# Sharing the attention normalisation between two engines, and taking the context rows of the MLP into products of quarters

## The chip, the cores and the metric

One core of one Trainium2 chip runs the whole program. The core has a matrix engine (TensorE; PE in the profile, with PEld for its weight loads), two engines for elementwise work (VectorE, shown as DVE, and ScalarE, shown as ACT), GpSimd (POOL), and SyncE (SP), which issues the DMAs. The metric is the device time of one execution in microseconds, the median over repeated runs.

## What is computed

Two layers of a hybrid transformer block over 512 latent tokens and 256 context tokens of width 1024. Cut to the two places that the change touches:

```python
# attention, per block of 128 query tokens; 8 query heads on 2 key/value heads, head size 64
p = softmax(concat([s_lat, s_ctx, s_sink], -1))           # keys: up to 3 latent blocks of 128, 2 context blocks
out = p_lat @ v_window + p_ctx @ v_ctx
...
# MLP, for the 512 latent rows in both layers, for the 256 context rows in layer 0 alone
f = square(relu(t @ w1)) @ w2                              # w1: 1024 x 4096, w2: 4096 x 1024
```

All matrix products run to single-precision accuracy by splitting: an operand x becomes a rounded part hi and a remainder lo = x - hi, and a product takes three matmuls, hi*hi + hi*lo + lo*hi.

## The kernel before, in words

The program is written in one order, and a planner then places the instructions of each engine: it follows the program with estimated costs and puts on each engine what is ready by them; of several that are ready it doesn't always take the one that stands first in the program. What it fixes is each engine's order; on the chip an engine executes that order and waits where an operand isn't there.

**Attention** (`phase_a`). A unit is one block of 128 query tokens with one key/value head, so four query heads. Layer 0 has 12 units (two context blocks first, then four latent ones), layer 1 has 8. `attn_scores` makes the four heads' scores in PSUM, adds the mask and takes the row maximum on VectorE (L936), takes exp with row sums on ScalarE (L944), then forms 1/sum on VectorE (L946, L947) and scales the four score tiles by it on VectorE (L949). `attn_values` transposes the scaled tiles on TensorE (L962), copies the transposed blocks from PSUM to the SBUF tile `pts`, on ScalarE for even and VectorE for odd blocks (L963; a ScalarE copy shows as L569, the line of the helper), and multiplies them with the values (L969). `pts` is one tile of up to five blocks in one buffer. Scores have two buffers a head (`np3` = 8), and the values of a unit run one unit behind its scores (`vlag` = 1). The output projection of finished blocks (`pass0`, and the products of `mm3`, L640 to L642) fills TensorE between them.

**MLP of layer 0** (`phase_mlp`). The 4096 hidden columns are worked in 8 groups of 512. Groups 3 to 6 are `strassen(g)`. There `up` makes the hidden tile of one 128-column chunk c, for the latent rows (24 matmuls of 512 columns) and the context rows (24 of 256). Then the down-projection of the latent rows runs as seven products of quarters in place of eight: `w2_forms` makes sums and differences of the four quarters of w2 and splits them (L666, L671, L672), `h_forms` does the same for the quarters of the latent hidden tile (L699, L700, L706 to L708, L712), and `times` multiplies a pair (L1507 to L1509, 12 matmuls of 512 columns), accumulating in the PSUM banks X, Y, Z, and adds the bank to the result `facc` (L1516) before the next product goes on in the same bank. The context rows go another way: `up` splits them (L1480, L1481) and `plain` multiplies them with the four quarters of w2 as they are, 24 matmuls and two adds (L1492) for each half of the columns. One `plain` stands ahead of the products X and Y, the other behind Y. The quarters of w2 live in 10 weight tiles that the w1 blocks of the group also use, so a form of w2 is made only when `up` or an earlier product gives tiles back.

## Time and profile before

| | |
|---|---|
| median of 3 runs | 1626.89 us (1626.73 to 1628.28) |
| the profiled execution | 1627.44 us, of which the trace spans 1625.7 us |
| TensorE busy | 1522.6 us, 94% |
| VectorE busy | 1078.5 us, 66% |
| ScalarE busy | 639.2 us, 39% |
| attention of layer 0, of layer 1 (about) | 245 to 362 us, 1155 to 1236 us |
| groups 3 to 6 of the MLP of layer 0 (about) | 635 to 907 us |

A busy TensorE isn't TensorE at its peak, since matmuls are pipelined and their ends are modelled; how much work fits in a stretch is read from the distance between the starts of matmuls. The share of busy time is a mean over stages with different limits, so each stage has to be read by itself.

### The profile page before, as it was taken

How to read it: one execution, taken by the hardware profiler on the slowest of the kernel's cores; microseconds unless marked ns; L12 is line 12 of the kernel's file. 1: busy time of each engine (PE TensorE's matmuls, PEld its weight loads, DVE VectorE, ACT ScalarE, POOL GpSimd, SP SyncE). 2: the span in 40 equal slices, each digit the busy share in tenths (PEclk: the TensorE clock that was granted, in tenths of full speed). 3: DMA queues.
4: the chain of work that ended last, by engine and by line, in shares of the span. 5: the costliest groups of instructions: out<-in, count | busy, mean ns of one | idle time of the engine just before them, and what ended most of it. 6: DMA issues, size and time to landing. Idle time of an engine off the chain costs nothing.

```text
span 1625.7 us, 22752 instructions
## 1 busy us (share of the span) xinstructions
PE 1522.6 (94%) x8740; PEld 1232.8 (76%) x8740; DVE 1078.5 (66%) x2288; ACT 639.2 (39%) x1199; POOL 188.0 (12%) x185
## 2 busy tenths in 40 slices
PE   5899999899999999999999997999889799999997
PEld 2677776667888888887888875688677688888885
DVE  8766638667885472647466476563763878879785
ACT  5411235654523121443334344122463564445441
POOL 0000121002312110000000135003201100000012
PEclk9999999999999999999999998879999899999999
DMA  9366412005232253042230347743302243232312
GB/s 346 120 209 207 151 46 79 1 21 187 73 134 93 76 178 100 29 132 102 106 130 2 121 186 295 266 143 93 117 1 104 104 155 104 89 119 85 123 59 84
DMA packets 72765, 193.82 MB, mean 119 GB/s; under 512 B 14928, under 2 KB 25424, under 8 KB 72272
## 3 DMA queue, kind: packets, MB, share of 16 engines
q1 hardware_dynamic: 68208, 188.17, 33.3%
q10 hardware_dynamic: 4448, 4.19, 0.8%
q8 instruction: 69, 1.13, 0.3%
q14 instruction: 40, 0.33, 0.1%
HBM read 172.15 MB, written 20.19 MB: 118 GB/s over the span
## 4 chain that ended last, share of the span: by engine, by line
PE 79%; DVE 11%; DMA 4%; ACT 4%; issue 1%; SPq 0%; POOL 0%; DVEq 0%; ACTq 0%
PE ps_m L640 15%; PE ps_m L641 15%; PE ps_m L642 15%; PE ps_q L1507 4%; PE ps_q L1508 4%; PE ps_q L1509 4%; PE ps_a L827 3%; PE ps_q L641 3%; PE ps_q L640 3%; PE ps_q L642 3%; ACT p L944 2%; PE ps_s L526 2%; DVE p L936 1%; PE ps_t L969 1%; DVE p L949 1%
## 5 line engine op out<-in xcount | busy, mean ns | idle before, releaser
L623 ACT CAST w<-w 128x1024 fp32r<-128x1024 f32 x128 | 133.8, 1049 | 221.6 <-PE ps_q L641 72.5
L641 PE MATMUL ps_m<-g,w 128*128 128x256 f32 (+1 forms) x544 | 178.6, 330 | 0.0
L640 PE MATMUL ps_m<-g,w 128*128 128x256 f32 (+1 forms) x544 | 177.0, 330 | 1.2 <-DVE g L784 1.2
L624 POOL TENSOR_TENSOR w<-w 128x1024 fp32r<-128x1024 f32 x33 | 80.6, 2443 | 839.4 <-ACT w L623 411.9
L642 PE MATMUL ps_m<-g,w 128*128 128x256 f32 (+1 forms) x544 | 177.5, 328 | 0.0
L641 PE MATMUL ps_m<-f,w 128*128 128x512 f32 (+1 forms) x464 | 170.0, 367 | 0.3 <-POOL f L787 0.3
L642 PE MATMUL ps_m<-f,w 128*128 128x512 f32 (+1 forms) x464 | 170.2, 368 | 0.0
L640 PE MATMUL ps_m<-f,w 128*128 128x512 f32 (+1 forms) x464 | 170.2, 371 | 0.0
L624 DVE TENSOR_TENSOR w<-w 128x1024 fp32r<-128x1024 f32 x95 | 120.1, 1267 | 74.8 <-ACT w L623 68.2
L640 PE MATMUL ps_m<-w,f 128*128 128x512 f32 (+1 forms) x400 | 147.6, 373 | 8.9 <-DVE p L989 4.0
L642 PE MATMUL ps_m<-w,f 128*128 128x512 f32 (+1 forms) x400 | 147.7, 370 | 0.0
L641 PE MATMUL ps_m<-w,f 128*128 128x512 f32 (+1 forms) x400 | 146.8, 368 | 0.0
L1516 DVE TENSOR_TENSOR g<-g,ps_q 128x512 f32<-128x512 f32 x146 | 93.4, 681 | 31.3 <-PE ps_q L1509 30.9
L641 PEld LDWEIGHTS ps_m<-g,w 128*128 128x128 f32 x544 | 104.0, 191 | 11.2 <-issue 1.2
L640 PEld LDWEIGHTS ps_m<-g,w 128*128 128x128 f32 x544 | 103.2, 192 | 11.7 <-DVE g L784 1.5
L642 PEld LDWEIGHTS ps_m<-g,w 128*128 128x128 f32 x544 | 103.8, 191 | 9.5 <-DVE w L624 0.4
L640 PEld LDWEIGHTS ps_m<-f,w 128*128 128x128 f32 x464 | 88.8, 193 | 19.6 <-issue 6.2
L642 PEld LDWEIGHTS ps_m<-f,w 128*128 128x128 f32 x464 | 88.9, 192 | 17.7 <-issue 4.5
L641 PEld LDWEIGHTS ps_m<-f,w 128*128 128x128 f32 x464 | 88.8, 191 | 14.6 <-DVE ssm_tab L303 1.2
L640 PEld LDWEIGHTS ps_m<-w,f 128*128 128x128 f32 x400 | 75.9, 190 | 22.7 <-issue 3.6
L640 PE MATMUL ps_q<-w,f 128*128 128x512 f32 x224 | 87.7, 395 | 2.3 <-DVE g L1682 2.0
L641 PE MATMUL ps_q<-w,f 128*128 128x512 f32 x224 | 87.8, 393 | 0.0
(319 smaller groups left out, 3256.3 us busy)
## 6 DMA issues: line engine op xcount, KB each, us to landing
w<-in_w_ada SPq DMA_DIRECT2D x72, 512.0 KB
w<-in_w_mlp_in SPq DMA_DIRECT2D x64, 512.0 KB
w<-in_w_mlp_out SPq DMA_DIRECT2D x36, 512.0 KB
wr<-in_w_mlp_out SPq DMA_DIRECT2D x14, 1024.0 KB
ada_w<-in_w_ada SPq DMA_DIRECT2D x21, 512.0 KB
w<-in_w_out SPq DMA_DIRECT2D x16, 512.0 KB
w<-in_w_conv SPq DMA_DIRECT2D x12, 512.0 KB
h_d<-g SPq DMA_DIRECT2D x12, 512.0 KB
```

The lines of the kernel that those rows point to most:

```text
L526: nc.tensor.matmul(out(g), U[d].o[rows, q, k].rearrange("p t i -> p (t i)"), sp[d][rows, q, k, lo:NCH], start=False, stop=d == 1 and q == ...
L623: nc.scalar.copy(hi, raw)
L624: (nc.gpsimd if turn % 2 and E.wpool and pool else nc.vector).tensor_sub(lo, raw, hi.bitcast(F32))
L640: nc.tensor.matmul(out, lh, rh, start=first, stop=False)
L641: nc.tensor.matmul(out, lh, rl, start=False, stop=False)
L642: nc.tensor.matmul(out, ll, rh, start=False, stop=last)
L827: nc.tensor.matmul(pa[32 * b:32 * b + 32, k * 256:(k + 1) * 256], E.cT[:, kc], raw[k][:, b * 256:(b + 1) * 256], start=kc == 0 and k == 0, ...
L944: nc.scalar.activation(p[i][:, :nk * P], p[i][:, :nk * P], AF.Exp, bias=nm[:, i:i + 1], accum_out=sm[:, i:i + 1])
L1507: nc.tensor.matmul(o, f[:, 0, c, js], rh[:, c], start=first and c == 0, stop=False, **kw)
L1508: nc.tensor.matmul(o, f[:, 0, c, js], rl[:, c], start=False, stop=False, **kw)
L1509: nc.tensor.matmul(o, f[:, 1, c, js], rh[:, c], start=False, stop=c == 1, **kw)
L1516: V.tensor_add(a_, a_, b_)
```

## The change

Three edits. In `attn_scores` the odd two of a unit's four tiles are scaled on ScalarE, the even two stay on VectorE. In `attn_values` each transposed block has a tile of its own, from nine buffers. In groups 3 to 6 of the MLP the context rows go through the same seven products as the latent rows: `h_forms` is run a second time on the context hidden tile (quarters of 128 rows), `times` makes a product of 6 matmuls for them behind each latent one, in a bank from the tag 'm' of three, and adds it to `facc`; `plain`, the split in `up` and the form r12 of w2 go. `up` now makes the latent rows of a chunk first. The new forms live in a pool that takes the place of the pool `prep`, whose work is drained first.

```diff
...
 
 
-def w2_forms(E, views, ctx):
+def w2_forms(E, views):
 
...
     yield "r11", split((0, 0))
     yield "r21", split((1, 0))
-    if ctx:
-        yield "r12", split((0, 1))
     yield "r22", split((1, 1))
...
 
 
-def h_forms(E, hf):
+def h_forms(E, hf, n, end, alloc):
 
 
     nc = E.nc
     V = nc.vector
-    q = {(i, j): hf[j][:, :, i * 256:(i + 1) * 256] for i in range(2) for j in range(2)}
+    q = {(i, j): hf[j][:, :, i * n:(i + 1) * n] for i in range(2) for j in range(2)}
 
     def split(x):
-        f = E.f4([P, 2, 2, 256], F32R)
+        f = alloc([P, 2, 2, n], F32R)
         nc.scalar.copy(f[:, 0], q[x])
         V.tensor_sub(f[:, 1], q[x], f[:, 0].bitcast(F32))
         return f
 
-    yield "l11", split((0, 0))
-    yield "l12", split((0, 1))
-    yield "l22", split((1, 1))
+    yield "l11" + end, split((0, 0))
+    yield "l12" + end, split((0, 1))
+    yield "l22" + end, split((1, 1))
     V.tensor_add(q[1, 1], q[1, 0], q[1, 1])
     V.tensor_sub(q[1, 0], q[0, 0], q[1, 0])
     V.tensor_sub(q[0, 0], q[1, 1], q[0, 0])
-    yield "s2", split((0, 0))
-    yield "s1", split((1, 1))
-    yield "s3", split((1, 0))
+    yield "s2" + end, split((0, 0))
+    yield "s1" + end, split((1, 1))
+    yield "s3" + end, split((1, 0))
     V.tensor_sub(q[0, 1], q[0, 1], q[0, 0])
-    yield "s4", split((0, 1))
+    yield "s4" + end, split((0, 1))
 
...
     V.reciprocal(sm, sm)
     for i in range(4):
-        V.tensor_scalar(out=p[i][:, :nk * P], in0=p[i][:, :nk * P], scalar1=sm[:, i:i + 1], scalar2=None,
-                        op0=OP.mult)
+        if i % 2:
+            nc.scalar.mul(p[i][:, :nk * P], p[i][:, :nk * P], sm[:, i:i + 1])
+        else:
+            V.tensor_scalar(out=p[i][:, :nk * P], in0=p[i][:, :nk * P], scalar1=sm[:, i:i + 1], scalar2=None,
+                            op0=OP.mult)
     return p, keys
...
     V = nc.vector
     nk = len(keys)
-    pts = E.ap.tile([P, 5, 512], F32, name="pts", tag="pts", bufs=1)
+    pts = []
     for j in range(nk):
         pt = E.pt('t')
         for i in range(4):
             nc.tensor.transpose(pt[:, i * P:(i + 1) * P], p[i][:, j * P:(j + 1) * P], E.ident)
-        (V.tensor_copy if j % 2 else E.copy)(pts[:, j], pt)
+        pts.append(E.ap.tile([P, 512], F32, name="pts", tag="pts", bufs=9))
+        (V.tensor_copy if j % 2 else E.copy)(pts[j], pt)
     po = E.pt('t')
     for j in range(nk):
         vv = v[:, keys[j], kv * 64:(kv + 1) * 64]
-        pr = pts[:, j].rearrange("p (a e t) -> p a e t", a=2, e=2)
+        pr = pts[j].rearrange("p (a e t) -> p a e t", a=2, e=2)
         for e in range(2):
...
         phase_a(E, l, cols, st)
     with psum_phase(E, f"m{l}", m=3, a=1, q=2) as E.pp, \
-            tc.tile_pool(name=f"mlp{l}", bufs=1, reuse_waits="tile") as E.g4p, \
-            tc.tile_pool(name=f"prep{l}", bufs=1, reuse_waits="tile") as E.mp:
+            tc.tile_pool(name=f"mlp{l}", bufs=1, reuse_waits="tile") as E.g4p, ExitStack() as E.late:
+        E.mp = E.late.enter_context(tc.tile_pool(name=f"prep{l}", bufs=1, reuse_waits="tile"))
         E.ps, E.nb4 = 'a', 2
...
         S = Env()
         S.hf = [E.f4([P, 2, NL]) for _ in range(2)]
-        S.hx = [E.f4([P, 4, NCX], F32R) for _ in range(2)] if both else None
+        if both:
+            hx = E.f4([P, 4, NCX])
+            S.hx = [hx[:, 2 * j:2 * j + 2] for j in range(2)]
         S.w, S.F = [], {}
...
         s = E.g4p.tile([P, 512], F32, name="relu", tag="relu", bufs=2)[:, :n]
         nc.scalar.activation(s, pt, AF.Relu)
-        nc.scalar.activation(s if sg else S.hf[c // 2][:, c % 2, ts], s, AF.Square)
-        if sg:
-            nc.scalar.copy(S.hx[0][:, c], s)
-            V.tensor_sub(S.hx[1][:, c], s, S.hx[0][:, c].bitcast(F32))
-
-    def plain(S, hf):
-
-        cs = slice(hf * 512, (hf + 1) * 512)
-        for t in (4, 5):
-            js = slice((t % 4) * P, (t % 4 + 1) * P)
-            pt = E.pt('m')
-            for c in range(4):
-                r = S.F[f"r{c // 2 + 1}{hf + 1}"]
-                mm3(nc, pt, S.hx[0][:, c, js], S.hx[1][:, c, js], r[0][:, c % 2], r[1][:, c % 2], c == 0, c == 3)
-            V.tensor_add(facc[t][:, cs], facc[t][:, cs], pt)
+        nc.scalar.activation((S.hx if sg else S.hf)[c // 2][:, c % 2, ts], s, AF.Square)
 
     begun = set()
 
     def times(S, bank, l, r, first, i, n):
 
         cs = slice(n * 512, (n + 1) * 512)
-        if bank not in S.F:
-            S.F[bank] = E.pt('q')
-        f, (rh, rl) = S.F[l], S.F[r]
-        for th in range(2):
-            o = S.F[bank][:, th * 512:(th + 1) * 512]
-            js = slice(th * P, (th + 1) * P)
+        rh, rl = S.F[r]
+
+        def product(o, f, js):
             kw = dict(skip_group_check=True)
             for c in range(2):
                 nc.tensor.matmul(o, f[:, 0, c, js], rh[:, c], start=first and c == 0, stop=False, **kw)
                 nc.tensor.matmul(o, f[:, 0, c, js], rl[:, c], start=False, stop=False, **kw)
                 nc.tensor.matmul(o, f[:, 1, c, js], rh[:, c], start=False, stop=c == 1, **kw)
-        for th in range(2):
-            t = 2 * i + th
+
+        def add(t, b_):
             if t not in facc:
                 facc[t] = E.g4([P, D])
-            a_, b_ = facc[t][:, cs], S.F[bank][:, th * 512:(th + 1) * 512]
+            a_ = facc[t][:, cs]
             if (t, n) in begun or both:
                 V.tensor_add(a_, a_, b_)
             else:
                 V.tensor_copy(a_, b_)
                 begun.add((t, n))
 
+        if bank not in S.F:
+            S.F[bank] = E.pt('q')
+        parts = [S.F[bank][:, th * 512:(th + 1) * 512] for th in range(2)]
+        for th in range(2):
+            product(parts[th], S.F[l], slice(th * P, (th + 1) * P))
+        for th in range(2):
+            add(2 * i + th, parts[th])
+        if both:
+            if bank + "c" not in S.F:
+                S.F[bank + "c"] = E.pt('m')
+            product(S.F[bank + "c"], S.F[l + "c"], slice(0, P))
+            add(4 + i, S.F[bank + "c"])
+
     def forms(S, g, n):
 
         if n:
-            S.R, S.L = w2_forms(E, w2[g * 4:g * 4 + 4], both), h_forms(E, S.hf)
-        for x in (S.R, S.L):
+            S.R, S.L = w2_forms(E, w2[g * 4:g * 4 + 4]), [h_forms(E, S.hf, 256, "", E.f4)]
+            if both:
+                lx = lambda s, d: E.mp.tile(s, d, name="lx", tag="lx", bufs=6)
+                S.L.append(h_forms(E, S.hx, 128, "c", lx))
+        for x in [S.R] + S.L:
             for k in range(n or 9):
...
             next(prep, None)
         for c in range(4):
+            up(S, c, 0)
             up(S, c, 1)
-            up(S, c, 0)
         forms(S, g, 3)
         forms(S, g, 0)
-        plain(S, 0)
         times(S, "X", "l11", "r11", True, 0, 0)
         times(S, "Y", "l12", "r21", True, 0, 0)
-        plain(S, 1)
         late_products(S)
...
             continue
         if l == 0 and g in E.fast:
+            if g == E.fast[0]:
+                drain(prep)
+                E.late.close()
+                E.mp = E.late.enter_context(E.tc.tile_pool(name="lx", bufs=1, reuse_waits="tile"))
             strassen(g)
```

## Rows read from the trace of the kernel before

**Rows 1.** The page: busy time of two engines, and the chain that ended last.
```profile
PE 1522.6 (94%) x8740; PEld 1232.8 (76%) x8740; DVE 1078.5 (66%) x2288; ACT 639.2 (39%) x1199; POOL 188.0 (12%) x185
PE 79%; DVE 11%; DMA 4%; ACT 4%; issue 1%; SPq 0%; POOL 0%; DVEq 0%; ACTq 0%
```

**Rows 2.** Busy time by stretch: length, then PE, PEld, DVE, ACT, POOL, clock, DMA.
```profile
245.00:362.00 117.00, 105.37 (x653) 79.70 (x652) 85.06 (x244) 68.68 (x181) 13.75 (x9) 0.97 0.11 35
1155.00:1236.00 81.00, 72.29 (x460) 55.11 (x460) 57.08 (x152) 47.41 (x119) 5.26 (x4) 0.96 0.11 40
637.00:668.50 31.50, 31.50 (x184) 26.49 (x183) 8.55 (x13) 12.24 (x26) 0.00 (x0) 1.00 0.31 101
668.50:706.00 37.50, 37.50 (x184) 29.77 (x183) 31.20 (x49) 16.59 (x27) 0.00 (x0) 1.00 0.25 85
```

**Rows 3.** Chain that ended last, by line: 245 to 365, 1150 to 1240.
```profile
by line: ACT p L944 15.4%; PE ps_t L969 11.9%; DVE p L936 10.5%; DVE p L949 9.6%; PE ps_t L962 5.5%; PE ps_m L642 4.2%; issue 4.2%; PE ps_m L640 4.1%; PE ps_m L641 3.8%; DVE pts L963 3.4%; DVE qs L911 2.8%; PE ps_q L932 2.3%; PE ps_q L934 2
by line: DVE p L936 12.3%; DVE p L949 10.8%; ACT p L944 10.7%; PE ps_t L969 9.6%; PE ps_t L962 8.8%; DVE pts L963 5.1%; PE ps_m L640 5.1%; PE ps_m L642 4.4%; PE ps_m L641 4.1%; DVE qs L911 3.8%; PE ps_q L932 3.8%; issue 3.2%; PE ps_q L933 2
```

**Rows 4.** One unit in order of time, VectorE: start, length, instruction, idle before.
```profile
319.99 0.16 DVE L941 TENSOR_TENSOR st<-st,nsink 128x4 f32<-128x4 f32 x1
...
323.48 0.16 DVE L946 TENSOR_TENSOR st<-st 128x4 f32<-128x4 f32 x1 [0.52 <-ACT p L944]
...
325.25 1.94 DVE L949 TENSOR_SCALAR p<-p,st 128x640 f32<-128x640 f32 x4
...
330.27 0.16 DVE L941 TENSOR_TENSOR st<-st,nsink 128x4 f32<-128x4 f32 x1
```

**Rows 5.** Groups on VectorE by shape, 245 to 365: count, busy us, mean ns, idle.
```profile
L949 DVE TENSOR_SCALAR p<-p,st 128x512 f32<-128x512 f32 x16 | 6.7, 480 | 0.1
```

**Rows 6.** Scaling by a column on ScalarE elsewhere: ns min/median/max, starts, forms.
```profile
L1207 ACT ACTIVATE f<-f,vecs x6: 510/722/723, 110.8 to 1061.1; 128x512 f32<-128x512 f32 x4, 128x256 f32<-128x256 f32 x2
L745 ACT ACTIVATE g<-g,rs x10: 1132/1140/1154, 393.8 to 997.5; 128x1024 f32<-128x1024 f32 x10
```

**Rows 7.** What VectorE's copies to pts (L963) waited for, whole run: us, times.
```profile
  PE ps_t L962: 15.4, 19
```

**Rows 8.** Waits of TensorE in 1140 to 1240: us in total, times, longest.
```profile
PE ps_q L932 <- DVE st L936: 4.5, 6, 1.7
PE ps_t L962 <- DVE pts L963: 2.5, 4, 0.8
```

**Rows 9.** Matmuls of 512 columns in order of time, ten starts apart.
```profile
784.43 0.39 PE L640 MATMUL ps_m<-f,w 128*128 128x512 f32 x1
...
786.69 0.39 PE L641 MATMUL ps_m<-f,w 128*128 128x512 f32 x1
```

**Rows 10.** Groups 3 to 6 by line (590 to 960): ns min/median/max, starts, forms.
```profile
L641 PE MATMUL ps_m<-w,f x64: 389/389/499, 668.7 to 886.2; 128*128 128x512 f32 x64
L1481 DVE TENSOR_TENSOR f<-relu,f x16: 421/425/428, 640.4 to 866.3; 128x256 fp32r<-128x256 f32 x16
```

**Rows 11.** VectorE in the products of group 3, in order of time.
```profile
669.12 1.29 DVE L672 TENSOR_TENSOR w<-w 128x512 fp32r<-128x512 f32 x2 [4.17 <-ACT w L671]
...
676.85 1.28 DVE L1516 TENSOR_TENSOR g<-g,ps_q 128x512 f32<-128x512 f32 x2
678.06 1.28 DVE L672 TENSOR_TENSOR w<-w 128x512 fp32r<-128x512 f32 x2
...
688.28 0.68 DVE L1492 TENSOR_TENSOR g<-g,ps_m 128x512 f32<-128x512 f32 x1
...
690.98 1.28 DVE L1516 TENSOR_TENSOR g<-g,ps_q 128x512 f32<-128x512 f32 x2 [2.02 <-PE ps_q L1509]
```

**Rows 12.** TensorE there: end of `up`, end of `plain`, first s2 matmul.
```profile
668.27 0.39 PE L642 MATMUL ps_m<-f,w 128*128 128x512 f32 x1
...
685.38 0.39 PE L642 MATMUL ps_m<-w,f 128*128 128x512 f32 x1
...
686.26 0.49 PE L1507 MATMUL ps_q<-w,f 128*128 128x512 f32 x1
```

## The prediction

> **What bounds the kernel now.** The page comes first: TensorE is busy for 94% of the span and carries 79% of the chain that ended last [rows 1]. So time is only to be had where TensorE does less work, or where it now stands idle. The busy time by stretch says where that is [rows 2]. In groups 3 to 6 of the MLP TensorE has no idle time (31.50 of 31.50 us, 37.50 of 37.50 us); there only fewer matmuls help. In the attention stretches it is idle for 117.00 - 105.37 = 11.6 us in layer 0 and 81.00 - 72.29 = 8.7 us in layer 1; these 20.3 us are the most that attention can give. The same view shows the danger: VectorE is nearly empty while `up` runs (8.55 of 31.50 us) and nearly full while the products run (31.20 of 37.50 us).
>
> What holds TensorE up in attention is read from the chain within the two stretches [rows 3]: it goes to and fro between the exps on ScalarE (L944), the maxima on VectorE (L936) and the scaling on VectorE (L949). L949 holds 9.6% of 120 us and 10.8% of 90 us, 11.5 + 9.7 = 21.2 us. One unit shows why [rows 4]. From the end of one L941 to the next is 10.28 us: the exps follow the first of them, L946 follows the last exp at 323.48, the scaling takes 1.94 us from 325.25, and only behind it in VectorE's queue come the next unit's last maxima, L941 and its exps. In layer 1 TensorE waits longest for those maxima (4.5 us), then for the copies to `pts` (2.5 us) [rows 8].
>
> **The change, part by part.**
>
> **Scaling on two engines.** A unit's four scalings take 1.94 us on VectorE where five key blocks are read, 0.485 us each [rows 4]; with four blocks an instruction is 0.48 us long by itself [rows 5]. Two of four go, so VectorE gets through a unit 0.97 us sooner with five blocks and about 0.85 with four. Over the 16 latent units that is some 14.5 us of VectorE time. The chain's own share says less: half of L949's 21.2 us is 10.6 us. I take 10.6 as the upper end. ScalarE gets two instructions a unit that no row shows in this place; the nearest are scalings by a column elsewhere, 0.72 us for 512 columns and 1.14 us for 1024 [rows 6], so 640 columns come to 0.72 + 128 x (1.14 - 0.72) / 512 = 0.83 us, and two to 1.4 to 1.7 us. They may start when the reciprocal is there (325.25 in the unit shown), a stretch in which ScalarE does not yet run the next exps (they begin at 330.27, behind L941). And the values stand one unit behind the scores, so that the transposes don't at once wait for the slower half. The ScalarE load bears it: 68.68 of 117 us plus 24 instructions of 0.4 to 0.83 us (about 15 us) makes 84. What is late next is TensorE: in the steady units it has about 1 us of idle time in ten (8.7 to 11.6 us in 8 to 12 units), so a loop that is 0.85 to 0.97 us shorter meets TensorE's own work at once. I take about six tenths of 10.6, 6 us, because ramps at both ends of a stretch and waits for the copies of transposed blocks are in the 20.3 us too and aren't cured by this. The lower end lies below nothing: if the 1.4 to 1.7 us stood ahead of copies that TensorE waits for in half of the 16 latent units, by the difference of 0.5 to 0.7 us, it would cost 4 us.
>
> On the unit price the Trainium skill (ScalarE: Activation LUTs, Rules for kernel authors) speaks against the edit: for multiplications it says to use VectorE and not ScalarE. The rows agree on the price, 0.72 us against 0.48 us for the same 512 columns. By the rule alone the moved half would cost about 0.25 us more for each instruction than it saves; that decides only if ScalarE is the engine waited for, which is the third rival below.
>
> **Single tiles for transposed blocks.** Nine buffers take away a wait of the copies for the previous unit's values. No such wait is in the trace: where VectorE stood idle before a copy, it was for the transposes L962 (15.4 us, 19 times), never for L969 [rows 7]. I cost it at nothing, with up to 2 us of gain as the bound, since a freer order might shorten the waits for these copies (2.5 us in layer 1) [rows 8].
>
> **Fewer matmuls.** Matmuls of 512 columns start 2.26 us / 10 = 0.226 us apart [rows 9]. `plain` has 48 of them in a group (one of its three lines runs 64 times in four groups) [rows 10]; the seven context products have 7 x 6 = 42. Six fewer in each of four groups are 24 x 0.226 = 5.4 us, on an engine without idle time: a gain in full, if nothing else becomes late.
>
> **What VectorE does in exchange, for each group.** Gone: the two subtractions for r12 at 0.60 us (a pair takes 1.29 us, the second starts 0.60 later) [rows 11], and four adds of `plain` at 0.60, the same size. New: seven adds of 128x512 at 0.60, and for the context forms seven splits and four combinations of 256 columns, 0.35 to 0.43 us each (0.43 is L1481 by itself [rows 10], 0.35 the same with the overlap of about 0.08 that the pairs show). Sum in the products: -1.2 - 2.4 + 4.2 + 11 x 0.36 = +4.6 us. The splits that go from `up` (L1481) gave VectorE time only where it was nearly empty. Against it, about 2.2 us can move ahead of the products: without r12 a pair of differences of w2 (1.2 us) waits for nothing there, and with the latent rows first, the first forms (some 1 us) are ready during the last context chunk. Net +2.4 us on a stretch in which VectorE ran from 669.12 to about 688.9 without a pause and again from 690.98 [rows 11].
>
> **What is late next.** Before, `plain` gave cover: from the end of `up` (668.5, its last matmul starts at 668.27) to the first product of s2 and t2 (686.26 [rows 12]) TensorE had 48 + 24 matmuls, 16.3 us, and a few matmuls of the next layer's modulation. Now X and Y with their context parts are 36 matmuls, 8.1 us. What VectorE must do before s2 and t2 can go on in bank X: splits of l12 and l22 1.2, three combinations 2.1 (0.7 each, since each needs the one before), s2 0.6, r22 1.2, a difference 1.2, t2 1.2, the adds of X 1.2, l12 of the context 0.36: 9.1 us. The latent matmuls end one context chunk before the end of `up`, 24 matmuls of half the columns at some 0.113, 2.7 us; relu, square and the first cast follow, three ScalarE instructions at 0.6 to 0.7 (the nearest row is 0.72 [rows 6]). So VectorE begins about 0.8 us ahead of the end of `up` (an estimate), and 8.3 us of work stand against 8.1 us of cover: even, if VectorE did these first and never waited. It won't quite: r22 gets its weight tiles only when `up` ends, t2 only when both uses of r11 are over (4.1 us later), and other ready forms stand between. From there to the last product VectorE has about 18 us more (adds 7.8, t1, t3, t4 3.6, other forms 4.6, a difference 1.2, part of the adds of Y), against 90 matmuls or 20.3 us on TensorE. I take 1.2 us of stall for a group, 4.8 us in all. Bounds: nothing (all hidden), and 4.6 us a group, 18.4 us, if all those other forms, which nobody needs yet, stood ahead. That forms do hold up an add shows in the trace: the last matmul of `plain` starts at 685.38, and its add runs at 688.28 [rows 11, 12], 2.5 us after that matmul is over.
>
> The order of `up`, the closing of `prep` (its seven steps are drawn in groups 1 and 2, long over) and ScalarE's smaller casts have cover: ScalarE is busy for 16.59 of 37.50 us [rows 2]. I cost them at nothing; if the new pool had to wait, it would be once, under 2 us.
>
> **Sum.** -6 (attention) - 5.4 (matmuls) + 4.8 (stalls) = -6.6 us. Against the profiled execution's own 1627.44 us that is 1620.8; the median of the runs is 0.55 us lower, so 1620.3, rounded to 1620.5 us, 0.4% faster.
>
> **The rivals.** A measurement of this kernel can tell about 0.2%, 3.3 us, from no change.
> First, **everything pays**: VectorE keeps up in the products (no stall, -5.4) and attention gives 9 to 10.6: 1611 to 1613 us. For it speaks that VectorE is free for 22.95 of 31.50 us while `up` runs; against it that the weight tiles keep the forms from going there.
> Second, on the other side, **VectorE holds up bank X**: with `plain` gone, the adds of X and the forms of t2 and s2 queue behind other forms that are ready, and TensorE stands still between Y and the third product, with no weights of the next group to go on with. It decides from a stall of 3.5 us a group, where 14 - 5.4 eats the 6 of attention and more; at 4 us a group it is +10.6 - 5 = 1632 us. For it: the 2.5 us in the trace, and the halved cover. Against: the count above is even, and the adds held up there were ones that no matmul was waiting for.
> Third, **ScalarE gives it back**: the two scalings lie in front of ScalarE's copies and casts, the loop is as long as before, and the products come out even: 1626 to 1628 us, no change. For it: ScalarE already holds the largest share of the chain in layer 0 (15.4%) [rows 3]; the Trainium skill's rule above points the same way. Against: its idle stretch just after the reciprocal.
>
> **Chances.** My forecast (1616 to 1623) 0.40, everything pays 0.18, no change 0.20, VectorE holds up bank X 0.22. So faster 0.58, same 0.20, slower 0.22. The range takes in the upper rival's time and the second's, to 1634 (4.6 us of stall): 1611 to 1634.
>
> **What would show it.** In the profile after: the matmuls L1507 to L1509 rise and `plain` is gone, 24 fewer of 512 columns. L949 has 40 instructions, and 40 scalings stand on ScalarE at 0.4 to 0.83 us. The attention stretches are 2 to 4 us shorter each, with more of the chain on TensorE. In the products TensorE shows waits for VectorE (adds, t2, s2) of about 1 us a group. I would be wrong if those waits were over 3 us a group, if attention were not shorter, or if the context products waited for a PSUM bank.

## The result, and the profile after

The changed kernel takes 1647.28 us (median of 4 runs, 1644.13 to 1652.1) against 1627.39 us for the kernel before: a ratio of 1.0121, with an interval of 1.0099 to 1.0144. It is 1.2% slower. The forecast was 1620.5 us in a range from 1611 to 1634, so both the sign and the range were wrong. The profiled execution took 1649.28 us, of which the trace spans 1647.5.

The page of the changed kernel, busy time by engine and the chain that ended last (answers to [rows 1]):

```profile
PE 1526.6 (93%) x8716; PEld 1231.2 (75%) x8716; DVE 1074.4 (65%) x2280; ACT 663.9 (40%) x1243; POOL 186.3 (11%) x185
PE 77%; DVE 12%; ACT 5%; DMA 4%; issue 2%; POOL 0%; SPq 0%; DVEq 0%; ACTq 0%
```

TensorE runs 24 matmuls fewer, 8716 for 8740, as the change promises, and yet it is busy for 4 us longer, in a span that is 21.8 us longer. ScalarE's busy time grew by 24.7 us.

Now by stage. Busy time by stretch (length, then PE, PEld, DVE, ACT, POOL, granted clock, DMA): first attention of layer 0 and of layer 1, from the first row maximum to the last matmul of the values, then the products of group 3.

```profile
240.00:370.50 130.50, 115.83 (x701) 88.09 (x699) 83.28 (x231) 84.58 (x208) 17.65 (x14) 0.95 0.09 31
1165.50:1258.00 92.50, 80.02 (x499) 59.91 (x499) 57.44 (x152) 61.40 (x139) 7.93 (x6) 0.94 0.13 46
...
675.90:706.00 30.10, 28.40 (x130) 20.99 (x129) 28.62 (x51) 12.94 (x24) 0.00 (x0) 1.00 0.27 88
```

In the kernel before, the same two stretches of attention lie from 236.8 to 364.0 and from 1148 to 1238:

```profile
236.80:364.00 127.20, 115.18 (x702) 87.47 (x700) 90.36 (x255) 70.35 (x185) 16.99 (x13) 0.96 0.10 32
1148.00:1238.00 90.00, 78.34 (x503) 59.38 (x501) 65.13 (x168) 51.04 (x124) 8.24 (x6) 0.96 0.13 48
```

Attention is 3.3 us longer in layer 0 and 2.5 us longer in layer 1. The starts of these stretches tell of the rest of the 21.8 us: layer 0's begins 3.2 us later than before (240.0 for 236.8), 11.0 us come between the two stretches, 8.6 of them in groups 3 to 6 (below), and 1.8 us behind the second. The 3.2 us ahead of attention are no more than kernels differ by whose program is that of before up to there: at the same matmul near 200 us e8 stands 2.9 us behind the kernel before, e12 1.6 us ahead.

In the two stretches VectorE has the relief that the change gives it (90.36 to 83.28 us, 65.13 to 57.44), ScalarE has the load, and the stretch didn't get shorter. In the products TensorE, which stood still nowhere before [rows 2], is idle for 1.7 of 30.1 us in group 3.

One unit of layer 0 with five key blocks, VectorE of the changed kernel in order of time (answers to [rows 4]; L950 is the scaling, L934 the maxima, L939 takes the place of L941):

```profile
326.82 0.16 DVE L939 TENSOR_TENSOR st<-st,nsink 128x4 f32<-128x4 f32 x1
...
331.77 1.02 DVE L950 TENSOR_SCALAR p<-p,st 128x640 f32<-128x640 f32 x2
333.27 0.82 DVE L934 CUSTOM_DVE_ANT_0 p<-ps_q,mask 128x640 f32<-128x640 f32 x1 [0.48 <-PE ps_q L933]
...
336.68 0.16 DVE L939 TENSOR_TENSOR st<-st,nsink 128x4 f32<-128x4 f32 x1
```

In this unit the scaling on VectorE fell from 1.94 to 1.02 us as planned. In two of the four units of this shape in layer 0 it didn't; the two tiles took as long as four before, while GpSimd worked beside them:

```profile
315.69 2.05 DVE L950 TENSOR_SCALAR p<-p,st 128x640 f32<-128x640 f32 x2
...
315.94 2.96 POOL L1361 TENSOR_TENSOR f<-f,f 128x512 f32<-128x512 f32 x2 [37.65 <-ACT dump L717]
```

In the unit shown first the cycle from L939 to L939 is 336.68 - 326.82 = 9.86 us; from one unit's first exp to the next it is 336.68 - 326.37 = 10.3 us, as in the kernel before (330.27 - 319.99 = 10.28). Behind the shorter scaling VectorE waits for TensorE's scores (0.48 us for L933). On ScalarE the scaling by itself has the sizes that were forecast; here are two of its groups in layer 0 (count, busy us, mean ns, idle):

```profile
L948 ACT ACTIVATE p<-p,st 128x640 f32<-128x640 f32 x8 | 6.2, 822 | 1.9 <-DVE st L945 1.9
L948 ACT ACTIVATE p<-p,st 128x512 f32<-128x512 f32 x8 | 5.3, 716 | 0.9 <-DVE st L945 0.9
```

Once TensorE stands still for the scaling on ScalarE itself. At the start of attention in layer 1 ScalarE has four scalings in a row, and the transposes of the scaled tiles wait 2.28 us for them; in the kernel before no transpose there waits for a scaling:

```profile
1177.37 2.54 ACT L948 ACTIVATE p<-p,st 128x512 f32<-128x512 f32 x4
...
1178.13 1.30 PE L963 MATMUL ps_t<-ident,p 128*128 128x128 f32 x6 [2.28 <-ACT p L948]
```

Groups 3 to 6: all that TensorE waited for there, in us, times and longest (the kernel before waits 0.2 us in this stretch).

```profile
PE ps_q L1494 <- DVE g L1503: 6.2, 4, 2.3
PE ps_q L1496 <- DVE f L698: 2.5, 3, 1.2
PE ps_q L1495 <- DVE w L672: 0.4, 2, 0.2
```

That is 9.1 us, 2.3 us a group. From the last matmul of group 2 to one and the same matmul of group 7 the kernel before takes 274.74 us, the changed one 283.36, 8.6 us more (the first two lines are of the kernel before):

```profile
633.37 0.39 PE L642 MATMUL ps_q<-w,f 128*128 128x512 f32 x1
908.11 0.28 PE L642 MATMUL ps_m<-g,w 128*128 128x256 f32 x1
...
640.76 0.39 PE L642 MATMUL ps_q<-w,f 128*128 128x512 f32 x1
924.12 0.28 PE L642 MATMUL ps_m<-g,w 128*128 128x256 f32 x1
```

TensorE's order of time shows what it waits for, in group 3 first and then in group 6:

```profile
685.96 0.50 PE L1494 MATMUL ps_q<-w,f 128*128 128x512 f32 x1
686.29 0.40 PE L1495 MATMUL ps_q<-w,f 128*128 128x512 f32 x1
687.49 0.47 PE L1494 MATMUL ps_q<-w,f 128*128 128x512 f32 x1 [0.80 <-DVE g L1503]
688.60 0.50 PE L1496 MATMUL ps_q<-w,f 128*128 128x512 f32 x1 [0.64 <-DVE f L698]
...
893.99 0.47 PE L1494 MATMUL ps_q<-w,f 128*128 128x512 f32 x1 [2.32 <-DVE g L1503]
895.70 0.79 PE L1496 MATMUL ps_q<-w,f 128*128 128x512 f32 x1 [1.24 <-DVE f L698]
```

The first two matmuls are of s2 and t2 in bank X. The third is the first matmul of the product in bank Z (s1 and t1), which the planner set between them. There are two banks of this kind, so Z has the place of Y, and its first matmul waits until VectorE has added Y. VectorE does that only after the forms that it has in front (L672 splits a quarter of w2, L666 takes a difference of quarters, L704 at 256 columns is the first sum of the context forms):

```profile
683.92 0.68 DVE L672 TENSOR_TENSOR w<-w 128x512 fp32r<-128x512 f32 x1
684.52 0.68 DVE L666 TENSOR_TENSOR w<-w 128x512 f32<-128x512 f32 x1
685.12 0.41 DVE L704 TENSOR_TENSOR f<-f 128x256 f32<-128x256 f32 x1
685.46 0.68 DVE L672 TENSOR_TENSOR w<-w 128x512 fp32r<-128x512 f32 x1
686.06 1.27 DVE L1503 TENSOR_TENSOR g<-g,ps_q 128x512 f32<-128x512 f32 x2
...
687.86 1.28 DVE L698 TENSOR_TENSOR f<-f,f 128x512 fp32r<-128x512 f32 x2
```

The add ends at 687.33 and the matmul starts at 687.49. TensorE executes its order as it stands, so the ten matmuls of bank X behind that one wait too. But the early place of Z's matmul is not what costs the time: the next one of X (L1496) needs the low half of s2, whose split (L698) VectorE makes behind the add of Y, in group 3 from 687.86, and L1496 waits once more until 688.60. So it is in groups 4 and 6 (in group 6 until 895.70); in group 5 sixteen small matmuls of the modulation run in between. With VectorE's order as it is, X would have stood about as long without Z's matmul ahead of it.

The third thing that changed is TensorE's clock. The trace shows two levels of the clock, 2.4 and 1.2 GHz. Each run lists its mean granted clock as a share of the upper one, and span x (1 - clock) is the most that the lower level can have cost, since TensorE isn't at work in all of that time: 53.6 us in the profiled execution before (0.967), 62.6 us after (0.962). As means over the runs it is about 50 us for the kernel before (49 to 51.5 in the groups of runs below) and 62.1 us for the changed one, so up to 12 us of the 20. The profile shows one place. The first four units of layer 0 work on context rows; the changed kernel there, in two stretches of 12 us, and then the kernel before, with the clock as the number behind POOL:

```profile
251.00:263.00 12.00, 7.09 (x34) 4.29 (x32) 9.77 (x33) 9.79 (x31) 4.04 (x3) 0.76 0.41 144
263.00:275.00 12.00, 10.99 (x53) 8.52 (x54) 5.75 (x21) 6.88 (x23) 0.00 (x0) 0.82 0.26 94
```

```profile
249.00:261.00 12.00, 8.99 (x38) 5.76 (x36) 10.33 (x34) 7.49 (x23) 4.48 (x3) 0.72 0.55 180
261.00:273.00 12.00, 11.33 (x68) 8.60 (x68) 9.41 (x36) 6.87 (x24) 0.25 (x1) 1.00 0.22 71
```

TensorE was busy for 7.09 of 12 us where it had been busy for 8.99; the clock then stands at 1.2 GHz for 10.2 us (before: 6.8) and falls once more at 301.5 for 3.4 us. The kernel before has a fall of 3.4 us at 236.4 that the changed one doesn't have, so in this attention it is 13.6 us against 10.2, and the clock can account for 1.7 us at most of the 3.3.

### The profile page after: what moved, and what is told of

Its sections match the earlier page's. It is cut to its first block, busy times and chain, and to the rows that moved or that the text cites. A ratio compares the mean times of both kernels' runs of the same rounds, so it can differ in the third digit from the quotient of the medians.

```text
span 1647.5 us, 22730 instructions
## 1 busy us (share of the span) xinstructions
PE 1526.6 (93%) x8716; PEld 1231.2 (75%) x8716; DVE 1074.4 (65%) x2280; ACT 663.9 (40%) x1243; POOL 186.3 (11%) x185
## 4 chain that ended last, share of the span: by engine, by line
PE 77%; DVE 12%; ACT 5%; DMA 4%; issue 2%; POOL 0%; SPq 0%; DVEq 0%; ACTq 0%
PE ps_m L640 15%; PE ps_m L641 14%; PE ps_m L642 14%; PE ps_q L1496 4%; PE ps_q L1494 4%; PE ps_q L1495 4%; PE ps_q L640 3%; PE ps_q L641 3%; PE ps_q L642 3%; PE ps_a L825 2%; PE ps_t L971 2%; ACT p L942 2%; PE ps_s L526 2%; PE ps_t L963 2%; DMA w<-in_w_ada 1%
## 5 line engine op out<-in xcount | busy, mean ns | idle before, releaser
L640 PE MATMUL ps_m<-w,f 128*128 128x512 f32 (+1 forms) x336 | 122.9, 368 | 11.6 <-ACT f L974 5.1
L642 PE MATMUL ps_m<-w,f 128*128 128x512 f32 (+1 forms) x336 | 122.6, 366 | 0.0
L641 PE MATMUL ps_m<-w,f 128*128 128x512 f32 (+1 forms) x336 | 121.6, 363 | 0.0
L640 PE MATMUL ps_q<-w,f 128*128 128x512 f32 x224 | 87.6, 395 | 2.3 <-DVE g L1687 2.0
L641 PE MATMUL ps_q<-w,f 128*128 128x512 f32 x224 | 87.9, 393 | 0.0
L642 PE MATMUL ps_q<-w,f 128*128 128x512 f32 x224 | 87.6, 392 | 0.0
```

The costliest lines, as they stand in the source:

```text
L640: nc.tensor.matmul(out, lh, rh, start=first, stop=False)
L641: nc.tensor.matmul(out, lh, rl, start=False, stop=False)
L642: nc.tensor.matmul(out, ll, rh, start=False, stop=last)
```

## The experiments

Each kernel ran beside the kernel before on the same chip (medians of 1627.9 to 1629.9 us in the six groups of runs). "Clock" and "rest" split the difference of the means over the runs: the change of span x (1 - granted clock), and the change of span x granted clock. So "clock" is the most that the clock can have cost, and it doesn't tell whether a low clock is a cause or follows from TensorE standing still. The clock is listed to 0.001, 1.6 us in one run, so these two are good to about 1 us.

| run | median us (range, runs) | ratio, interval | clock, rest |
|---|---|---|---|
| e1_norm | 1641.78 (1638.72 to 1645.84, 4) | 1.0087, 1.0065 to 1.0109 | +9.6, +3.3 |
| e2_pts | 1626.95 (1623.01 to 1632.29, 10) | 0.9994, 0.9979 to 1.0009 | -0.1, -1.2 |
| e3_ctx | 1638.58 (1635.22 to 1639.06, 4) | 1.0061, 1.0044 to 1.0078 | +5.0, +3.8 |
| e4_attn | 1641.18 (1637.66 to 1645.48, 4) | 1.0083, 1.006 to 1.0106 | +9.2, +3.1 |
| e5_scale_pool | 1641.41 (1639.37 to 1644.68, 4) | 1.008, 1.0057 to 1.0102 | +8.2, +4.7 |
| e6_scale_latent | 1636.75 (1632.64 to 1642.31, 5) | 1.0042, 1.0021 to 1.0063 | +8.1, +0.4 |
| e7_forms_pool | 1638.36 (1633.26 to 1645.21, 10) | 1.0059, 1.004 to 1.0078 | +2.7, +6.6 |
| e8_forms_order | 1643.43 (1642.25 to 1647.92, 4) | 1.0095, 1.0073 to 1.0117 | +5.0, +10.4 |
| e9_odd_unscaled | 1626.13 (1620.8 to 1630.86, 10) | 0.9972, 0.9957 to 0.9987 | -2.3, -1.6 |
| e10_none_scaled | 1626.21 (1621.14 to 1631.94, 10) | 0.998, 0.996 to 1.0 | -1.1, -3.2 |
| e11_same_load | 1639.63 (1629.66 to 1645.35, 10) | 1.0057, 1.0033 to 1.0081 | +3.1, +6.3 |
| e12_ctx_no_vector | 1621.18 (1620.1 to 1623.2, 4) | 0.9943, 0.9924 to 0.9962 | -2.8, -5.8 |
| e13_ctx_first | 1635.19 (1632.98 to 1645.69, 10) | 1.0042, 1.0025 to 1.006 | +1.5, +4.8 |
| e14_share_no_copies | 1632.69 (1628.23 to 1641.26, 10) | 1.0031, 1.0011 to 1.005 | +0.9, +2.8 |
| e15_copies_scalar | 1631.82 (1628.49 to 1636.85, 10) | 1.0019, 1.0003 to 1.0034 | +2.2, +0.3 |
| e16_ctx_mid | 1637.75 (1631.84 to 1643.66, 10) | 1.0051, 1.0031 to 1.007 | +3.4, +4.8 |
| e17_first_pool | 1634.91 (1632.34 to 1640.66, 11) | 1.0043, 1.0028 to 1.0059 | +0.8, +5.9 |
| e18_w2_early | 1634.42 (1629.61 to 1638.2, 10) | 1.0037, 1.0024 to 1.005 | +2.0, +4.4 |

### Which part of the change costs it

**e1_norm**: the kernel before with the shared scaling alone.

```diff
-        V.tensor_scalar(out=p[i][:, :nk * P], in0=p[i][:, :nk * P], scalar1=sm[:, i:i + 1], scalar2=None,
-                        op0=OP.mult)
+        if i % 2:
+            nc.scalar.mul(p[i][:, :nk * P], p[i][:, :nk * P], sm[:, i:i + 1])
+        else:
+            V.tensor_scalar(...)
```

> The kernel before with one part of the change alone: the odd two of a unit's four score tiles are scaled on ScalarE. Theory A (the attention stretches of the changed kernel are 3.1 and 3.2 us longer because ScalarE, which now holds the scalings, delays the copies and the exps that stand behind them): 1631 to 1635 us, with both attention stretches about 3 us longer than before. Rival B (the single tiles and the freer order of transposes that they allow cost it): 1622 to 1627 us here. As I forecast: 1621 us.

**e2_pts**: the single tiles alone.

```diff
-    pts = E.ap.tile([P, 5, 512], F32, name="pts", tag="pts", bufs=1)
...
+        pts.append(E.ap.tile([P, 512], F32, name="pts", tag="pts", bufs=9))
```

> The kernel before with one part alone: each transposed block has its own tile, nine buffers. Theory A: no change, 1626 to 1628 us, since no copy waited for the values of the unit before. Rival B: 1631 to 1635 us, since the planner puts transposes of a unit ahead of the values of the one before and TensorE stands behind them.

**e3_ctx**: the context part alone: the changed kernel with the two edits above taken back.

```diff
-        if i % 2:
-            nc.scalar.mul(p[i][:, :nk * P], p[i][:, :nk * P], sm[:, i:i + 1])
...
+    pts = E.ap.tile([P, 5, 512], F32, name="pts", tag="pts", bufs=1)
```

> The kernel before with one part alone: the context rows of groups 3 to 6 go through the products of quarters. Theory A (bank X and the forms of s2 and t2 wait for VectorE once plain is gone; the groups of the changed kernel take 8.6 us longer than before): 1635 to 1638 us, with TensorE waiting 2 to 6 us between Y and the third product of each group. Rival (the groups are as good as before and the loss of the changed kernel comes from the attention that hands over late): 1621 to 1627 us.

**e4_attn**: the edits of e1 and e2 together.

```diff
+            nc.scalar.mul(p[i][:, :nk * P], p[i][:, :nk * P], sm[:, i:i + 1])
...
+        pts.append(E.ap.tile([P, 512], F32, name="pts", tag="pts", bufs=9))
```

> The kernel before with both attention parts (scaling on two engines and single tiles), without the context part. Theory A: as the scaling alone, 1631 to 1635 us. Rival C (the two attention parts hurt only together, by the order that the planner makes of both): 1633 to 1636 us while each alone stays within 1625 to 1629 us.

e1 and e4 came out 7 and 5 us above what any of the theories allowed, e2 and e3 (to 0.6 us) where the first theory put them. By the medians scaling costs 13.1 us, the context part 9.9 us, single tiles nothing that can be told (-1.8). The sum of the three, 21.2, is about the whole, 19.9: the parts add up, and neither saves the other. Two separate causes are to be found.

Where e1's loss lies can be read by setting the same matmuls of both traces side by side. Its profiled run was the slowest of the four, 19.0 us behind at the last matmul: 3.4 us come ahead of attention, 6.3 from the start of attention to the MLP in layer 0, 4.0 between the MLP of layer 0 and attention in layer 1, 5.3 from there on. The first of these is within what runs differ by there without any change to the program (above); of the third, one profile doesn't tell.

### Scaling: the gain, and the taker's price

**e5_scale_pool**: the odd tiles go to GpSimd and not to ScalarE.

```diff
-            nc.scalar.mul(p[i][:, :nk * P], p[i][:, :nk * P], sm[:, i:i + 1])
+            nc.gpsimd.tensor_scalar(out=p[i][:, :nk * P], in0=p[i][:, :nk * P], scalar1=sm[:, i:i + 1], ...)
```

> The kernel before with the odd two of a unit's tiles scaled on GpSimd in place of ScalarE. VectorE is relieved as in the change, ScalarE gets nothing. Theory A (ScalarE's extra 0.5 to 0.8 us an instruction is what costs): 1625 to 1631 us, back near the kernel before. Rival D (the relief itself costs: with VectorE free earlier the planner puts the work that fills TensorE elsewhere, and the granted clock falls in the thinner stretches): 1636 to 1643 us, with 14 to 20 us of half clock between 230 and 375 against 10 before.

It was as slow as e1. I took that as proof that the relief of VectorE is itself the harm. That was too quick, as e9 shows. GpSimd has its own price; one of its groups, and one of VectorE's beside it:

```profile
L950 POOL TENSOR_SCALAR p<-p,st 128x640 f32<-128x640 f32 x8 | 16.0, 2016 | 29.9 <-DVE st L947 24.9 <-ACT f L1361 5.0
...
L953 DVE TENSOR_SCALAR p<-p,st 128x512 f32<-128x512 f32 x8 | 4.9, 656 | 0.1
```

2.0 us a tile, and VectorE's own tile of 512 columns takes 656 ns for 480 [rows 5].

**e6_scale_latent**: shared in the 16 latent units only; the four context units stay on VectorE.

```diff
-        if i % 2:
+        if i % 2 and lat:
```

> The kernel before with the scaling shared only in latent units; the four context units of layer 0 scale on VectorE as before. In the scaling run the first stretch of half clock in attention (from 256 us) was 13.7 us long against 6.8 before, and lay in these context units and the first latent one. Theory E (half of the loss sits there): 1633 to 1637 us, with that stretch back at about 7 us. Rival (the loss is spread over the latent units): 1639 to 1643 us.

Met: 5.0 us less than e1 by the medians, for four of 20 units. In its profile these four units run as in the kernel before (27.4 us from the first exp to the fifth unit's first, before 27.5), while e1 takes 30.5 us, with the clock at 1.2 GHz from 256.2 for 13.7 us. The other 8.7 us of loss stay with the sharing in the 16 latent units alone, by the split nearly all of it clock (+8.1, rest +0.4).

**e9_odd_unscaled**: the odd tiles stay unscaled, no engine takes them (this part of the softmax is left out).

```diff
-        V.tensor_scalar(out=p[i][:, :nk * P], ...)
+        if i % 2 == 0:
+            V.tensor_scalar(out=p[i][:, :nk * P], ...)
```

> The kernel before, with the scaling of the odd tiles left out altogether (they stay as the exponentials): VectorE scales two tiles of a unit, and no engine takes the other two. Load theory: what made sharing slow is the work that the other engine takes on, so with nobody taking it the time falls below before, 1617 to 1625. Order theory: VectorE's scaling isn't what ends the cycle of a unit, and the planner, which sees the tiles ready earlier, sets the filler matmuls elsewhere on TensorE, which costs as much as in the shared versions: 1635 to 1643.

**e10_none_scaled**: no tile is scaled (all of the normalisation is left out).

```diff
-    for i in range(4):
-        V.tensor_scalar(out=p[i][:, :nk * P], ...)
```

> The kernel before, with the scaling of all four tiles of a unit left out (21 us of VectorE's work in the trace of before). If VectorE's scaling bounded the units, as the prediction has it, this gives some 10 to 20 us: 1607 to 1618. If TensorE's own order sets the cycle, nothing is gained: 1628 or more, and by the order theory 1632 to 1643.

The order theory fell: without a taker nothing is lost, and e9 gains 0.28%, 4.6 us (3.3 by the medians). But leaving out the other half gains nothing more, and e10's interval reaches to no change. One unit of e10 shows why, VectorE in order of time:

```profile
323.78 0.17 DVE L941 TENSOR_TENSOR st<-st,nsink 128x4 f32<-128x4 f32 x1
...
330.55 0.82 DVE L936 CUSTOM_DVE_ANT_0 p<-ps_q,mask 128x640 f32<-128x640 f32 x1 [1.72 <-PE ps_q L935]
...
333.97 0.16 DVE L941 TENSOR_TENSOR st<-st,nsink 128x4 f32<-128x4 f32 x1
```

Without any scaling the cycle is 333.97 - 323.78 = 10.19 us; VectorE now stands 1.72 us for TensorE's scores. So the steady unit is not bound by VectorE's scaling. What closes it at 10.2 us isn't shown; TensorE is busy for 8.89 us of this cycle.

**e11_same_load**: shared as in e1, but VectorE multiplies the even tile once more, by 1, in place of each odd one.

```diff
+            V.tensor_scalar(out=p[i - 1][:, :nk * P], in0=p[i - 1][:, :nk * P], scalar1=1.0, ...)
```

> Scaling shared with ScalarE as in the changed kernel, but VectorE does as much work as before: in the place of each odd tile it multiplies the even one once more, by 1. Order theory: with VectorE as late as before the planner leaves TensorE's order nearer to before (92 of 7798 matmuls out of sequence against 227 in the shared version) and most of the loss goes: 1626 to 1634. Load theory (ScalarE's extra 0.7 us a tile delays its copies of the transposed blocks): as slow as the shared version or slower, 1639 to 1646.

1639.63: slow although VectorE is as loaded as before and TensorE's order nearer to before. Again against the order theory. The spread is wide, 1629.66 to 1645.35 us, and the clock goes with it: 0.974 in the fastest of these runs, 0.963 in the slowest.

**e14_share_no_copies**: shared as in e1, with all copies of transposed blocks on VectorE.

```diff
-        (V.tensor_copy if j % 2 else E.copy)(pts[:, j], pt)
+        V.tensor_copy(pts[:, j], pt)
```

> Scaling shared with ScalarE as in the changed kernel, and all copies of transposed blocks on VectorE instead of every other one on ScalarE, so that ScalarE's load of a unit is back where it was before (two scalings more, two or three copies less) and VectorE's is somewhat above before. Queue theory (what costs is ScalarE's queue, in which copies and exponentials come behind the scalings): most of the loss goes, 1626 to 1634. Hand-over theory (a tile scaled on another engine costs by itself): 1637 to 1645.

**e15_copies_scalar**: the kernel before with all these copies on ScalarE.

```diff
-        (V.tensor_copy if j % 2 else E.copy)(pts[:, j], pt)
+        E.copy(pts[:, j], pt)
```

> The kernel before with all copies of transposed blocks on ScalarE (one or two more a unit), and all scaling on VectorE as before: ScalarE gets as much more load as by the shared scaling and no scaling is handed over. Queue theory: as slow as the shared version or nearly, 1635 to 1645. Hand-over theory: about as before, 1626 to 1632.

Taking the copies off ScalarE brings the shared version from 1.0087 down to 1.0031, some 9 us of 14, nearly all of it clock (+9.6 to +0.9). That is what the queue theory said. e15 came out where the other theory put it. In e15 ScalarE has about as much more work in attention, 81.68 + 59.42 = 141.1 us against 146.0 after and 121.4 before, and the price is 0.19%, 3 us:

```profile
238.00:369.00 131.00, 116.65 (x704) 88.61 (x702) 80.19 (x237) 81.68 (x206) 17.50 (x13) 0.95 0.09 31
1155.00:1247.00 92.00, 79.99 (x505) 61.12 (x503) 54.33 (x152) 59.42 (x140) 8.50 (x6) 0.93 0.14 49
```

So ScalarE's load alone is not the price, and neither theory holds by itself: scalings and copies together on ScalarE cost what neither costs alone. That their place in the queue decides is argued, not shown; the one wait in the trace that is for a scaling is that of 2.28 us above. Which of the copies and exps behind a scaling hurts isn't settled.

### The context rows: VectorE in the products

**e7_forms_pool**: e3 with the sums, differences and splits of the context forms on GpSimd.

```diff
-    V = nc.vector
+    V = nc.gpsimd if end else nc.vector
```

> The context part alone, with the sums, differences and splits of the context forms on GpSimd, which does nothing in that stretch (0.00 us of 37.5 before). That takes about 4 us a group from VectorE. Theory A (VectorE's load between Y and the third product makes the stall): 1622 to 1630 us, the waits of TensorE for VectorE in groups 3 to 6 under 3 us in all, against 9 us. Rival (the banks or the order of TensorE make it): 1635 to 1639 us as with the forms on VectorE.

No gain by the median. The waits only changed their names. TensorE in groups 3 to 6:

```profile
PE ps_q L1492 <- DVE f L698: 3.0, 4, 0.7
PE ps_m L1491 <- DVE w L672: 2.9, 4, 1.0
PE ps_m L1490 <- DVE g L1499: 1.6, 2, 1.0
PE ps_q L1490 <- DVE g L1499: 0.9, 4, 0.2
```

8.4 us in place of 9.1. Between the two matmuls at the ends of groups 3 to 6 it takes 7.7 us more than before, e3 8.7.

**e8_forms_order**: e3 with the three streams of forms drawn in turn and not one after another.

```diff
-        for x in [S.R] + S.L:
-            for k in range(n or 9):
+        for k in range(n or 9):
+            for x in [S.R] + S.L:
```

> The context part alone, with the forms written in the order in which the products need them (w2, latent, context in turn, in place of all of w2, then all latent, then all context). The same work on the same engines. Theory F (what stalls is the order: forms that nobody needs yet stand ahead of those of s2 and t2): 1628 to 1633 us. Rival A (the load itself): 1635 to 1639 us.

This one failed to test what it was for. In groups 3 to 6 the planner gave TensorE the same order as in e3, with the same waits (6.2, 2.5 and 0.4 us). But layer 1 uses the same function, and there the order did change: behind attention in layer 1 (1306.8 us in the trace of before) e8 is 11.5 us behind the kernel before, at the last matmuls (1614.8) 15.9. It says nothing on the context rows.

**e12_ctx_no_vector**: e3 with VectorE's part of the context forms left out: no sums of quarters, and the low half of a form is a second ScalarE copy. The kernel leaves out the sums and the remainders of the context rows.

```diff
+        if end:
+            nc.scalar.copy(f[:, 1], q[x])
+            return f
         V.tensor_sub(f[:, 1], q[x], f[:, 0].bitcast(F32))
...
+    if not end:
         V.tensor_add(q[1, 1], q[1, 0], q[1, 1])
```

> The context part alone, with VectorE's work in the context forms left out: no sums of quarters, and the second half of each form is a ScalarE copy. VectorE still adds the products. Theory of the prediction (VectorE, loaded without pause behind the last chunk, holds up the context bank and the forms): the waits of TensorE in groups 3 to 6 for VectorE, 8.7 us, mostly go, and 24 matmuls fewer pay: 1622 to 1630. Rival (the adds alone, or the granted clock in these groups, cost it): 1635 to 1640.

1621.18 us, 17 us below e3 and 8 us below the kernel before. All that TensorE waited for in groups 3 to 6:

```profile
PE ps_q L1497 <- DVE f L701: 0.9, 2, 0.5
```

With eleven short VectorE instructions a group gone, the waits go and the 24 matmuls pay: between the two matmuls at the ends of groups 3 to 6 (here 631.64 and 901.19) it takes 5.2 us less than before, where 5.4 were forecast. The other 3 us lie outside the groups. The adds of the context products stayed, so they alone don't do it: with the chunks in this order, VectorE's context forms behind the last chunk are what costs the context part its gain.

**e13_ctx_first** and **e16_ctx_mid** keep the work and move it: the context chunks' forms are made beside the latent chunks.

```diff
         for c in range(4):
-            up(S, c, 0)
             up(S, c, 1)
+        S.F.update(h_forms(E, S.hx, 128, "c", lx))
+        for c in range(4):
+            up(S, c, 0)
         forms(S, g, 3)
```

> The context part alone, with the context chunks of a group made first and their forms directly behind them, ahead of the four latent chunks; all work is kept. Moment theory: VectorE makes the context forms beside the latent chunks, and behind the last chunk only the latent forms are left, as in the kernel before; TensorE's waits for VectorE behind the last chunk (8.7 us in four groups) shrink to those of the adds, and the 24 matmuls fewer pay: 1620 to 1630. Amount theory (VectorE is short of time in the whole group): 1634 to 1641.

In e16 the first two latent chunks stay among the context ones, and the forms come ahead of the last two:

```diff
+            if c < 2:
+                up(S, c, 0)
             up(S, c, 1)
+        S.F.update(h_forms(E, S.hx, 128, "c", lx))
+        for c in (2, 3):
+            up(S, c, 0)
```

> As e13_ctx_first, but the context chunks lie among the first two latent chunks as in the changed kernel and their forms come ahead of the last two latent chunks. Moment theory: 1620 to 1630 as well; amount theory: 1634 to 1641.

By the medians e13 gets back 4.5 of e3's 9.9 us and e16 2.0, but the intervals overlap that of e3. Between the two matmuls at the ends of groups 3 to 6 they take 6.2 and 6.5 us more than before, e3 8.7: about a quarter comes back. In e13 TensorE now waits at the context bank:

```profile
PE ps_m L1490 <- DVE g L1499: 4.8, 4, 1.6
PE ps_m L1491 <- DVE w L672: 4.0, 6, 1.7
```

8.8 us again. The context products now need the forms of w2 and the adds sooner than VectorE makes them.

**e17_first_pool**: e13 with the context forms on GpSimd as in e7.

```diff
+    V = nc.gpsimd if end else nc.vector
```

> The context part alone, with the context chunks first as in e13 and their forms' sums and differences on GpSimd, ahead of the four latent chunks; all work is kept. Amount theory: VectorE is as free as with its share left out (1621), GpSimd has the time of four latent chunks (some 22 us) for eleven operations of 1 us on each half, and the waits for VectorE behind the last chunk go: 1619 to 1628, which would beat the kernel before. Rival: GpSimd and VectorE slow each other down, or what is left of VectorE's work (the adds and the forms of w2) still holds up the banks: 1630 to 1640.

**e18_w2_early**: e17 with two forms of w2 drawn ahead of the third and fourth latent chunk.

```diff
+        S.R = w2_forms(E, w2[g * 4:g * 4 + 4])
         for c in range(4):
+            if c >= 2:
+                S.F.update([next(S.R)])
             up(S, c, 0)
```

> As e17_first_pool, with the first two of the seven forms of w2 (r11, r21) made ahead of the third and the fourth latent chunk instead of behind the last; all work is kept. Queue theory (behind the last chunk VectorE has the forms of w2, the latent forms and the adds at once, and TensorE waits for whichever is last): the waits for the forms of w2 and the adds shrink by half or more, 1624 to 1631. Rival (the buffers of the w2 forms come free only as the chunks end, so that nothing can be made earlier, or ScalarE's relu is held up behind them): 1634 to 1642.

Neither gets there. In e17 VectorE has no context form left, and still TensorE waits 4.7 us for the adds and 3.8 us for forms of w2; in e18 it is 4.7 and 3.9. Between the two matmuls at the ends of the groups they take 7.3 and 7.2 us more than before. So it isn't VectorE's sum of work alone. The order of the products may do it, but e13 and e16 to e18 also differ from e3 and e12 in another point: their latent chunks come last, so the last latent forms have no cover from a context chunk any more. In group 3 of e12 the last splits of the latent quarters start 0.6 us ahead of the last matmul of `up` (666.66), in e17 4.5 us behind it (663.77); one line of each:

```profile
666.06 1.29 DVE L701 TENSOR_TENSOR f<-f,f 128x512 fp32r<-128x512 f32 x2 [5.59 <-ACT f L697]
...
668.24 1.28 DVE L698 TENSOR_TENSOR f<-f,f 128x512 fp32r<-128x512 f32 x2
```

No run takes the two apart; a kernel with e12's order and all the work was not tried. None of the complete versions beats the kernel before.

## Why the prediction was wrong, point by point

Two terms of the sum failed. The scaling on two engines was put at a gain of 6 us, with a loss of 4 at the worst; it lost 13. The stall in the products was put at 1.2 us a group; it is 3.5.

**What bounds the kernel.** That there is no idle time in groups 3 to 6 and some 20 us in attention was right. That VectorE's scaling closes the loop of a unit was wrong: with none of it the unit still takes 10.19 us (e10). The chain of waits [rows 3] gave L949 21.2 us, and leaving all of L949 out gained 0.2%, 3 us. (The exps follow L940, at 330.07, and not L941, which starts with them at 330.27; no term hangs on that.) A share of the chain is what a line holds, not what is won when it goes.

**Scaling on two engines** (forecast -6, bounds -10.6 and +4; measured +13). The relief of VectorE was not so badly sized: half of the scaling taken away and given to nobody is worth 4.6 us (e9). What failed is the other side of the same step, the lower end: ScalarE's two instructions have the forecast length (0.82 and 0.72 us), but I let them cost at most 4 us, because ScalarE was idle just after the reciprocal in the unit that I looked at. That unit is a steady one, and its cycle indeed stayed at 10.3 us. Two steps behind the bound failed. I costed the 16 latent units and left out the four context units, which make 5 of the 13 us (e6 against e1). And I held that the transposes would not at once wait for the slower half, and gave TensorE's waits no price in clock: the transposes do wait, 2.28 us at the start of layer 1 (2.2 in e1, before nothing), and up to 9.6 of e1's 13 us are clock. How the 8.7 us that the latent units alone lose (e6) come about is open beyond that: e14 shows that scalings and copies together on ScalarE are needed for most of it, e15 that its load alone isn't enough. The relief, too, is less than counted: in two of the four units VectorE's two scalings take about 2.04 us beside GpSimd, and not 1.02. The Trainium skill (ScalarE: Activation LUTs, Rules for kernel authors), which says VectorE and not ScalarE for multiplications, points the right way. It isn't the unit price that decided, though: 13 us for 40 instructions are 0.33 us each, more than the 0.24 by which the unit prices differ, and e15 gave ScalarE nearly as much more work for 3 us.

**Single tiles** (forecast 0): right (e2).

**Fewer matmuls** (forecast -5.4): 24 are gone, and where hardly anything waits groups 3 to 6 are 5.2 us shorter (e12). Right.

**What is late next in the products** (forecast +4.8, at 1.2 us a group; bounds 0 and 4.6). TensorE's waits are 9.1 us, 2.3 a group. The groups as a whole are 8.6 us longer, although the matmuls give 5.4, so the price is (8.6 + 5.4) / 4 = 3.5 us a group. Beside the waits it holds the clock, which falls for 3.4 us in each of two groups (up to 3.4 us of the 14), and 1.5 us that no wait names. (By the medians of e3 it is (9.9 + 5.4) / 4 = 3.8.) So the bound held, and I took a value near the wrong end of it, by a count that let VectorE do first what is needed first. The second rival, "VectorE holds up bank X", which decides from 3.5 us, is what happened: X's third matmul waits for s2 until VectorE has got through the adds and forms in front of it. The list names Z for most of that wait, because the planner had set Z's first matmul, whose bank is Y's, in the middle of X.

**The third rival**, that ScalarE gives it back, had the right engine (e14) and was too mild: I let it bring attention back to no change, not to a loss.

**The sum.** +13 and +10 in place of -6 and -0.6, and -2 for the single tiles make 1628 + 21 = 1649, where 1647 was measured; the products' term alone was off by some 10 us, the scaling's by 19. Of the signs that the prediction named, the one for attention (not shorter) told against it at once; the one for the waits (over 3 us a group) did not, since clock and unnamed gaps took the rest.

## What to carry to other kernels

Before work is moved off an engine, leave it out altogether and time that: it gives the most that the move can bring, here 4.6 us, against which the taker's price then stands. A share of the chain of waits is no such measure where the cycle closes without that line at nearly the same length. And on engines that execute a fixed order a wait is listed under the first instruction that meets it, here Z's matmul; before it is blamed, look at what the next instruction needs, here a form that comes still later in VectorE's order. When cover is taken away (here `plain`, in e13 the context chunk behind the last latent one), count what stands in that order ahead of the first form that is needed, not only what is needed.
